# mLSTM's values and output gate as seven block products, with block differences of the normed activations kept in scratch

## The chip, the core and the metric

The kernel runs on one NeuronCore of a Trainium2 chip. Its engines work side by side, each through its own list of instructions in a fixed order: TensorE (PE in the profile, with PEld for the loading of its stationary operand), VectorE (DVE), ScalarE (ACT), GpSimd (POOL) and SyncE (SP, which here only issues DMA transfers). The metric is the device time of one execution in microseconds; the time of a kernel is the median of its runs.

## The reference

A decoder trunk of two layers over 512 tokens of width 1024, in float32. Each layer:

```
h = rmsnorm(x) * norm_mix
z = h @ w_in      # q, k, v of attention | q, k, v, o of mLSTM | i, f | gates A, B
att = sliding_window_attention(rope(qk_norm(q)), rope(qk_norm(k)), v)     # window 128
hm  = headnorm(mlstm(q_m, k_m, v_m, i, f)) * sigmoid(o_m)
x = x + (sigmoid(gA) * (att @ w_att_branch) + sigmoid(gB) * (hm @ w_m_branch)) @ w_out
x = x + relu(rmsnorm(x) * norm_ffn @ w_ff1)^2 @ w_ff2
```

`v_m` and `o_m` are each 512 wide, and their columns lie next to each other in `w_in` (`C_VM` 1280 and `C_OM` 1792). So h times these columns is one product of 512 x 1024 by 1024 x 1024.

## The kernel before

Every float32 operand of a projection is split into a high part, rounded to the matmul's float32r type, and a low part, the rest. `mm3` makes one product of three matmuls: high by high, high by low, low by high. Activations are split once (`norm.big`: two tiles of 128 x 8 x 512, features on the partitions). Weights are split chunk by chunk: `chunk` loads 128 rows by 512 columns on SP's queue into one of three raw buffers (`wraw`), ACT writes the high part (L195), DVE the low part (L196), into one of four pairs of buffers (`wsp`). `group_steps` turns a projection into 32 steps: 8 chunks times 4 output blocks of 128, three matmuls each, into four PSUM banks of 128 x 512. `banks` hands these out in pairs, named x, y and f, in turn. `tok_steps` leaves tokens on the output's partitions, `feat_steps` features.

The mixer of a layer is written as two `weave`s. A weave is a list of steps of matmuls, each with a width of 0.25 in a unit of its own (twelve matmuls make 1.0), and a list of side jobs with a position in that unit. Side jobs are attention, mLSTM, norms, transposes and `beat`s. The order on each engine is then fixed ahead of the run by a planner: it takes the work by priority as it expects it to be ready; `high_priority` brings a piece forward, and `issue_after` keeps it behind another on the same engine.

The first weave is attention's q, then its k and v with the gate logits (16 units). The second is, before: mLSTM's q and k (position 0), gates 0 and 1 (8 and 16), V with `ev_v` (24), the attention branch `a_steps` for both halves (32 and 36), gate 2 (40), O with `ev_o` (48), gate 3 (56 to 64). Attention's side jobs start at 7, one pair of query block and key head each 1.65. mLSTM's four heads start at 28 and each takes 4.65; `m_norm` follows, then `ev_o` multiplies the sigmoid of O into `hm`, and `head_tr` transposes and splits `hm` for the mLSTM branch, which comes behind the weave. The branches' product and `w_out` end the mixer.

`vm` holds V by token with a column of ones. It uses the buffer (`mid10`) of attention's keys `kT`. `xtok` holds x by token in four tiles of 128 x 2 x 512; the norm reads them at the mixer's start, and `ev_x` adds the mixer's result to them at its end.

The MLP makes most of its products by a scheme of seven block products: for a matrix product in 2 x 2 blocks, seven products of sums and differences of blocks stand in for eight. Sums of the weights' blocks are made by DMA in DRAM: class `Sums` copies one block with a DMA on ACT's queue (`copy`, L404) and adds another with an accumulating DMA on POOL's queue (`add`, L409, behind a small copy that marks the place, L407). These are jobs in a list; each `beat` sends one. The mixer's beats serve the MLP's sums of `w_ff2`.

Of the kernel before, what the change touches and what calls it, by code (L numbers as in the profile page):

```python
# [16 lines left out]
P = 128  # L17
# [18 lines left out]
def hybrid_kernel(ctx, tc, x, norm_mix, w_in, att_q_norm, att_k_norm, att_sinks, m_gate_bias,  # L36
# [39 lines left out]
    def temp(dt=F32):  # L76
        return now["tmp"].tile([P, T], dt, tag="t", name=nm("t"))
# [265 lines left out]
    xtok = [[const.tile([P, 2, T], F32, name=f"x{t}_{j}") for j in range(2)] for t in range(2)]  # L343
# [87 lines left out]
    def beats(*at):  # L431
        return [(a, beat) for a in at]

    def mixer(l, norm, late, order, phase):
# [20 lines left out]
        acts = norm.acts  # L455

# [7 lines left out]
        def ev_kv(b, ps):  # L464
# [5 lines left out]
              late + [(6.9, norm.columns), (10.0, lambda: row.append(norm.along()))])  # L470
# [283 lines left out]
        def ev_v(b, ps):  # L754
            if b == 0:
                vm.append(mid.tile([P, NB, MH, MV + 1], F32, tag="mid10", name=nm("vm")))
                gp.memset(vm[0][:, :, :, MV:], 1.0)
            sc.activation(vm[0][:, b, :, 0:MV], ps.rearrange("p (h v) -> p h v", h=MH), AF.Copy,
                          scale=norm.col[:, b:b + 1])
# [94 lines left out]
        side.append((28 + 4.65 * (MH + 1) + -0.55, m_norm))  # L854
# [4 lines left out]
        def head_tr(f):  # L859
            ps = aux()  # L860
            for b in range(NB):
# [450 lines left out]
```

## Time and profile before

| | |
|---|---|
| median of three runs | 1319.54 us (1313.72, 1319.54, 1320.67) |
| the profiled execution | 1317.72 us |
| its span, first to last instruction | 1316.0 us |
| mean granted clock of TensorE | 0.997 |
| first mixer's attention, mLSTM, branches | about 60 to 290 us of the span |
| first MLP | about 290 to 650 us |
| matmuls | 7126 |

The page shows shares of busy time, the chain of work that ended last, and groups of instructions by line. A matmul's duration in a group is longer than its share of TensorE's time, since a matmul begins before the one ahead of it has ended. Names such as mm<-i,wh say what is written and read: mm is a PSUM tile of a projection, i the split activations, wh and wl the parts of a weight chunk, aux a PSUM tile of attention, mLSTM or a transpose; a, t and u are buffers that several tensors use in turn, so mm<-u,wh in a mixer is the attention branch.

### The profile page before, as it was taken

How to read it: one execution, taken by the hardware profiler on the slowest of the kernel's cores; microseconds unless marked ns; L12 is line 12 of the kernel's file. 1: busy time of each engine (PE TensorE's matmuls, PEld its weight loads, DVE VectorE, ACT ScalarE, POOL GpSimd, SP SyncE). 2: the span in 40 equal slices, each digit the busy share in tenths (PEclk: the TensorE clock that was granted, in tenths of full speed). 3: DMA queues.
4: the chain of work that ended last, by engine and by line, in shares of the span. 5: the costliest groups of instructions: out<-in, count | busy, mean ns of one | idle time of the engine just before them, and what ended most of it. 6: DMA issues, size and time to landing. Idle time of an engine off the chain costs nothing.

```text
span 1316.0 us, 19614 instructions
## 1 busy us (share of the span) xinstructions
PE 1294.6 (98%) x7126; PEld 1112.5 (85%) x7126; DVE 967.1 (73%) x1507; ACT 782.5 (59%) x1393; POOL 228.8 (17%) x331
## 2 busy tenths in 40 slices
PE   9999999999999999999999999999999999999998
PEld 7877788888889989999888777888888899999987
DVE  4688764466578897978947887645757878979786
ACT  5568765544376656667544787564545766666663
POOL 4512311100011122220015023110001111213100
PEclk9999999999999999999999999999999999999999
DMA  5422136748287999776314222367483799997743
GB/s 153 111 71 72 57 101 153 178 129 241 59 199 184 265 181 221 189 176 199 104 35 122 63 75 63 105 154 174 135 241 52 189 239 229 185 258 147 190 145 128
DMA packets 139169, 196.52 MB, mean 149 GB/s; under 512 B 10424, under 2 KB 76576, under 8 KB 139072
## 3 DMA queue, kind: packets, MB, share of 16 engines
q1 hardware_dynamic: 93040, 135.88, 33.5%
q0 software_dynamic: 37568, 44.17, 22.0%
q10 hardware_dynamic: 8464, 15.21, 3.6%
q8 instruction: 56, 0.92, 0.3%
q14 instruction: 41, 0.34, 0.1%
HBM read 193.14 MB, written 31.46 MB: 171 GB/s over the span
## 4 chain that ended last, share of the span: by engine, by line
PE 82%; DVE 7%; issue 5%; DMA 3%; ACT 2%; POOL 0%; DVEq 0%; SPq 0%; POOLq 0%; ACTq 0%
PE mm L47 70%; PE aux L47 10%; DMA raw<-in_w_ff_dram 3%; PE aux L51 2%; DVE wl L196 2%; DVE t L646 1%; DVE t L696 1%; DVE wl L921 0%; ACT t L659 0%; ACT wh L195 0%; DVE t L623 0%; DVE a L725 0%; DVE a L876 0%; ACT wh L920 0%; DVE a L728 0%
## 5 line engine op out<-in xcount | busy, mean ns | idle before, releaser
L47 PE MATMUL mm<-i,wh 128*128 128x512 f32 (+1 forms) x1216 | 328.0, 357 | 4.6 <-DVE u L1153 4.6
L921 DVE TENSOR_TENSOR wl<-raw,wh 128x1024 fp32r<-128x1024 f32 x218 | 264.8, 1222 | 69.1 <-ACT wh L920 68.8
L920 ACT ACTIVATE wh<-raw 128x1024 fp32r<-128x1024 f32 x218 | 230.0, 1056 | 126.5 <-PE mm L47 57.2
L47 PEld LDWEIGHTS mm<-i,wh 128*128 128x128 f32 x1216 | 212.9, 192 | 31.3 <-DVE u L1153 5.0
L196 DVE TENSOR_TENSOR wl<-w,wh 128x512 fp32r<-128x512 f32 (+1 forms) x208 | 142.1, 684 | 119.3 <-ACT wh L195 111.9
L47 PE MATMUL mm<-i,wl 128*128 128x512 f32 (+1 forms) x608 | 215.5, 355 | 0.0
L195 ACT ACTIVATE wh<-w 128x512 fp32r<-128x512 f32 (+1 forms) x208 | 127.2, 612 | 145.2 <-PE mm L47 109.0
L47 PE MATMUL mm<-wh,uh 128*128 128x512 f32 x448 | 175.0, 391 | 0.0
L47 PE MATMUL mm<-wl,uh 128*128 128x512 f32 x448 | 174.8, 390 | 0.0
L47 PE MATMUL mm<-wh,ul 128*128 128x512 f32 x448 | 174.3, 389 | 0.0
L961 POOL DMA_DIRECT2D raw<-in_w_ff_dram x56 | 72.7, 1298 | 489.4 <-DVE wl L921 284.2
L47 PE MATMUL mm<-wh,i 128*128 128x512 f32 (+1 forms) x512 | 149.2, 369 | 0.2 <-ACT wh L195 0.2
L47 PEld LDWEIGHTS mm<-i,wl 128*128 128x128 f32 x608 | 116.6, 192 | 15.2
L47 PE MATMUL mm<-hs,wh 128*128 128x256 f32 x672 | 122.2, 283 | 0.3 <-ACT u L1149 0.3
L47 PEld LDWEIGHTS mm<-hs,wh 128*128 128x128 f32 x672 | 105.7, 192 | 1.7 <-ACT u L1149 0.5
L47 PEld LDWEIGHTS mm<-wh,i 128*128 128x128 f32 x512 | 91.5, 188 | 15.7 <-issue 0.7
L47 PEld LDWEIGHTS mm<-wh,ul 128*128 128x128 f32 x448 | 84.1, 188 | 18.0
L47 PEld LDWEIGHTS mm<-wh,uh 128*128 128x128 f32 x448 | 84.3, 188 | 16.3
L47 PEld LDWEIGHTS mm<-wl,uh 128*128 128x128 f32 x448 | 84.3, 188 | 16.0
L47 PE MATMUL mm<-hs,wl 128*128 128x256 f32 x336 | 95.1, 283 | 0.0
L47 PE MATMUL mm<-wl,i 128*128 128x512 f32 (+1 forms) x256 | 94.0, 367 | 0.0
L975 DVE SCALAR_TENSOR_TENSOR x<-mm,ninv,x 128x512 f32<-128x512 f32 x112 | 80.2, 747 | 18.5 <-PE mm L47 18.4
(246 smaller groups left out, 2198.1 us busy)
## 6 DMA issues: line engine op xcount, KB each, us to landing
raw<-in_w_ff_dram SPq DMA_DIRECT2D x124, 512.0 KB, 5.8
w<-in_w_in_dram SPq DMA_DIRECT2D x128, 256.0 KB, 2.7
raw<-in_w_ff_dram POOLq DMA_DIRECT2D x56, 512.0 KB, 7.2
sum<-in_w_ff_dram ACTq DMA_DIRECT2D x28, 512.0 KB, 5.0
raw<-sum SPq DMA_DIRECT2D x28, 512.0 KB, 4.2
sum<-in_w_ff_dram POOLq DMA_DIRECT2D x20, 512.0 KB, 6.4
w<-in_w_out_dram SPq DMA_DIRECT2D x32, 256.0 KB, 3.5
w<-in_w_att_branch_dram SPq DMA_DIRECT2D x16, 256.0 KB, 2.7
```

What stands on the lines that cost most here:

```text
L47: return nc.tensor.matmul(*args, **kw)
L51: return nc.tensor.transpose(*args)
L195: last_wh[:] = sc.activation(wh[:, :off], raw[:, :off], AF.Copy), wh
L196: ve.tensor_tensor(wl[:, :off], raw[:, :off], f32(wh[:, :off]), op=ALU.subtract)
L646: ve.copy_predicated(dst, tri_i.unsqueeze(1).to_broadcast([P, 2, P]), p4[:, :, 1, :])
L696: ve.tensor_tensor(b3[64 * i:64 * i + 64], p4[:, :, i, :], l4[:, :, i, :], op=ALU.add)
L920: last_wh[:] = sc.activation(hi, r, AF.Copy), hi[:, 0, :]
L921: ve.tensor_tensor(lo, r, f32(hi), op=ALU.subtract)
L961: nc.gpsimd.dma_start(r, w1_block(k, n, c0), accum_op=ALU.add)
L975: ve.scalar_tensor_tensor(xh[:, i, :], ps[i], norm.inv[:, 0 if sign > 0 else 1, b:b + 1], xh[:, i, :], op0=ALU.mult, op1=ALU.add)
```

## The change

V and O of a layer become one product in 2 x 2 x 2 blocks: two blocks of 256 tokens, two of 512 features, two of 512 columns (V and O). Seven block products take the place of eight. In the order in which they run they are 1, 2, 4, 5, 6, 7, 3. Each has four chunks of weights, two token blocks of 128 and three matmuls, that is 24 matmuls and a width of 2 in the weave; together 14 in the place of V (24 to 38), and O's place behind gate 2 is gone. Weights of 1, 2 and 3 are plain blocks; those of 4 to 7 are sums from DRAM, made by a `Sums` of its own in 16 jobs. Products 1, 2 and 4 take blocks of the split activations as they are. 5, 6, 7 and 3 take differences, which `left_steps` makes on DVE during the first weave and splits again on ACT and DVE. Those of 5 and 6 are kept in x's own tiles, those of 7 and 3 are written to DRAM by POOL and fetched into x's tiles when 5 and 6 are done. x itself comes back by four loads (`x_back`) from position 42.5, in layer 0 from the input, in layer 1 from copies in DRAM that POOL writes at the mixer's start.

The results add up in PSUM where they can (6 and 7 go on top of 1, 3 on top of 5) and otherwise in SBUF: `ev_vo` copies with ACT or adds with DVE. O's raw values wait in `oraw`, and `o_gate` takes their sigmoid behind `m_norm`. mLSTM's heads start at 32 instead of 28, and `head_tr` at 57.0.

```diff
-    xtok = [[const.tile([P, 2, T], F32, name=f"x{t}_{j}") for j in range(2)] for t in range(2)]
+    xpool = ctx.enter_context(tc.tile_pool(name="xpool", bufs=1, reuse_waits="tile"))
+
+    def x_tile(t, j, dt=F32):
+        return xpool.tile([P, 2, T], dt, tag=f"x{t}_{j}", name=nm(f"x{t}_{j}"))
+
+    xtok = [[x_tile(t, j) for j in range(2)] for t in range(2)]
...
+    def plan_vo(l):
+
+        s = Sums(l, 0, lambda l, _, i, j, h: w_in[l, T * i + 2 * P * h:T * i + 2 * P * (h + 1),
+                                                  C_VM + T * j:C_VM + T * (j + 1)])
+        jobs.extend(s.copies("DB") + s.adds("D") + s.copies("C") + s.adds("B") + s.copies("A") + s.adds("CA"))
+        return s
...
+        def x_back(t, j):
...
+            xtok[t][j] = x_tile(t, j)
+            nc.sync.dma_start(xtok[t][j], src)
...
+        if l:
+            for t in range(2):
+                for j in range(2):
+                    x_kept[t, j] = dram.tile([P, 2, T], F32, tag=nm("x"), name=nm("x"))
+                    gp.dma_start(x_kept[t, j], xtok[t][j])
+
+        def left_steps(at):
...
+            def whole(t, k):
+                r[t, k] = [temp(), temp()]
+                for d, (hi, lo) in zip(r[t, k], block(t, k)):
+                    ve.tensor_tensor(pair(d), f32(hi), f32(lo), op=ALU.add)
+
+            def keep(which, e):
+                if which in (5, 6):
+                    to = vo_left[which] = x_room(which)
+                    for n in range(2):
+                        h, lo = (v[:, 2 * n:2 * n + 2, :] for v in to)
+                        sc.activation(h, pair(r[e][n]), AF.Copy)
+                        ve.tensor_tensor(lo, pair(r[e][n]), f32(h), op=ALU.subtract)
+                    return
+                vo_left[which] = dram.tile([2, P, 2, T], F32, tag=nm("left"), name=nm("left"))
+                for n in range(2):
+                    hl = split(r[e][n], get=lambda: temp(F32R))
+                    for m in range(2):
+                        gp.dma_start(vo_left[which][m, :, n, :], f32(hl[m]))
...
+            return [(at, lambda: (whole(*a21), whole(*a22), minus(a22, a22, a21))), (at + 1, lambda: keep(5, a22)),
+                    (at + 2, lambda: (whole(*a11), minus(a22, a22, a11, -1.0))), (at + 3, lambda: keep(6, a22)),
+                    (at + 4, lambda: (minus(a21, a11, a21), keep(7, a21))),
+                    (at + 5.5, lambda: (whole(*a12), minus(a12, a22, a12, -1.0), keep(3, a12)))]
...
-              late + [(6.9, norm.columns), (10.0, lambda: row.append(norm.along()))])
+              late + [(6.9, norm.columns), (10.0, lambda: row.append(norm.along()))] + left_steps(7.2)
+              + beats(*(5 + 1.4 * n for n in range(8))))
...
+        def ev_vo(t, j, ps, add):
...
+            with tc.high_priority():
+                for i in range(2):
+                    b = 2 * t + i
+                    dst, src = oraw[t][:, i, :] if j else vm[0][:, b, :, 0:MV], ps[i]
...
+                    by = (mcol if j else norm.col)[:, b:b + 1]
+                    if add:
+                        ve.scalar_tensor_tensor(dst, src, by, dst, op0=ALU.mult, op1=ALU.add)
+                    else:
+                        sc.activation(dst, src, AF.Copy, scale=by)
+
+        def vo_steps():
+
+            ps, lefts = {}, {}
+            slots = [(1, "x", True, ((0, 0, False),)), (2, "z", True, ((0, 0, True),)),
+                     (4, "y", True, ((1, 0, False),)), (5, "z", True, ((1, 1, False),)),
+                     (6, "x", False, ((0, 1, False),)), (7, "x", False, ((1, 0, True), (1, 1, True))),
+                     (3, "z", False, ((0, 1, True),))]
...
+            def run(s, which, bank, fresh, evacs, kt, i, w):
...
+                mm3(ps[bank][i], ah[:, kt % 2, c], al[:, kt % 2, c], w[0], w[1], fresh and kt == 0, False,
+                    skip_group_check=True)
+                if kt == 3 and i == 1:
+                    for t, j, add in evacs:
+                        ev_vo(t, j, ps[bank], add)
+                    if which == 4:
+                        turn_of[0] -= 2
+                    elif which in (5, 6):
+                        fetch({5: 7, 6: 3}[which])
...
-        def ev_o(b, ps):
-            so = temp()
-            sc.activation(so, ps, AF.Sigmoid, scale=norm.col[:, b:b + 1])
-            ve.tensor_tensor(hm[b], hm[b], so, op=ALU.mult)
-            if b == NB - 1:
-                sigmoid(g2)
+        def o_gate():
+            for b in range(NB):
+                so = oraw[b // 2][:, b % 2, :]
+                sc.activation(so, so, AF.Sigmoid)
+                ve.tensor_tensor(hm[b], hm[b], so, op=ALU.mult)
+            sigmoid(g2)
...
-            at = 28 + 4.65 * h
+            at = 32 + 4.65 * h
...
-        side += [(57.75 + 1.25 * f, lambda f=f: head_tr(f)) for f in range(MH)]
+        side += [(57.0 + 1.1 * f, lambda f=f: head_tr(f)) for f in range(MH)]
...
-        side += beats(*(42 + 1.8 * n for n in range(12)))
-        weave(feat_steps(acts, wcols(C_QM, 512), ev_qk) + s0 + s1 + tok_steps(acts, wcols(C_VM, 512), ev_v)
-              + a_steps(0, g0) + a_steps(1, g1) + s2 + tok_steps(acts, wcols(C_OM, 512), ev_o) + s3, side)
+        side += [(42.5 + 2 * n, lambda n=n: x_back(n // 2, n % 2)) for n in range(4)]
+        side += beats(*(0.75 + 1.6 * n for n in range(8)), *(42 + 1.7 * n for n in range(12)))
+        weave(feat_steps(acts, wcols(C_QM, 512), ev_qk) + s0 + s1 + vo_steps()
+              + a_steps(0, g0) + a_steps(1, g1) + s2 + s3, side)
```

More of the change, by code (lines that the diff above doesn't have):

```diff
@@ L455, in mixer, with pair, block, x_room @@
         acts = norm.acts
+        vo_sums = plan_vo(l)
+        vo_left = {}
+        def pair(t):
+            return t.rearrange("p (k t) -> p k t", k=2)
+        def block(t, k):
+            return [tuple(b[:, 4 * k + 2 * n:4 * k + 2 * n + 2, 2 * P * t:2 * P * (t + 1)] for b in norm.big)
+                    for n in range(2)]
+        def x_room(which):
+            t = int(which in (6, 3))
+            return [x_tile(t, j, F32R).rearrange("p i (k t) -> p (i k) t", k=2) for j in range(2)]
@@ L752, in mixer @@
         vm = []
[L754 to L755 removed]
+        oraw = []
+        mcol = sm([P, NB], "mcol", 1)
+        ve.tensor_scalar(mcol, norm.col, -1.0, None, op0=ALU.mult)
+        def ev_vo(t, j, ps, add):
+            if not vm:
                 vm.append(mid.tile([P, NB, MH, MV + 1], F32, tag="mid10", name=nm("vm")))
                 gp.memset(vm[0][:, :, :, MV:], 1.0)
[L758 to L759 removed]
+            if j and not oraw:
+                oraw.extend(mid.tile([P, 2, T], F32, tag=tag, name=nm("o")) for tag in ("mid4", "kvi"))
+            with tc.high_priority():
+                for i in range(2):
+                    b = 2 * t + i
+                    dst, src = oraw[t][:, i, :] if j else vm[0][:, b, :, 0:MV], ps[i]
+                    if not j:
+                        src = src.rearrange("p (h v) -> p h v", h=MH)
+                    by = (mcol if j else norm.col)[:, b:b + 1]
+                    if add:
+                        ve.scalar_tensor_tensor(dst, src, by, dst, op0=ALU.mult, op1=ALU.add)
+                    else:
+                        sc.activation(dst, src, AF.Copy, scale=by)
```

43 lines of the change are left out of this document (42 added, 1 removed).

## The prediction

> **What bounds the kernel now.** I read the page's share of engines first, then the chain that ended last, then stretches of layer 0's mixer.
>
> ```profile
> span 1316.0 us, 19614 instructions
> PE 1294.6 (98%) x7126; PEld 1112.5 (85%) x7126; DVE 967.1 (73%) x1507; ACT 782.5 (59%) x1393; POOL 228.8 (17%) x331
> ...
> PE 82%; DVE 7%; issue 5%; DMA 3%; ACT 2%; POOL 0%; DVEq 0%; SPq 0%; POOLq 0%; ACTq 0%
> ```
>
> TensorE is busy in nearly all of the span and holds 82% of the chain; DVE holds 7%. What a matmul costs is not its mean of about 390 ns in the groups, since matmuls overlap. It is the step from one to the next, and a stretch of the chain without waits gives it (start, length, what):
>
> ```profile
> 230.34 20.45 PE mm L47 x90
> ```
>
> 20.45 / 90 = 0.2272 us for a 128x512 matmul. A projection of 96 such costs 21.8 us.
>
> Now the stretches, cut at the events that matter: the K/V stage and the attention's preparation (33 to 60), attention (60 to 163), mLSTM (163 to 230), the rest of the mixer.
>
> ```profile
> core 0: us, PE busy (x) PEld busy (x) DVE busy (x) ACT busy (x) POOL busy (x), PEclk, DMA share, GB/s
> 33.00:60.00 27.00, 27.00 (x166) 24.29 (x165) 17.92 (x41) 12.87 (x27) 13.07 (x22) 1.00 0.45 122
> 60.00:163.00 103.00, 98.34 (x480) 76.19 (x479) 84.98 (x204) 74.17 (x195) 28.58 (x53) 1.00 0.24 67
> 163.00:230.00 67.00, 66.97 (x342) 56.49 (x341) 37.88 (x111) 41.25 (x119) 9.79 (x22) 1.00 0.48 124
> 230.00:290.00 60.00, 60.00 (x276) 49.67 (x275) 33.27 (x58) 29.59 (x47) 3.72 (x6) 1.00 0.58 152
> ```
>
> From 163 on TensorE never waits, and DVE works 57% of the time. From 60 to 163 TensorE idles 4.7 us, and DVE is busy 84.98 / 103 = 82.5%. There the chain runs through attention, in turns on TensorE and DVE. Its end, and what TensorE does then:
>
> ```profile
> 156.73 0.69 DVE wl L196
> 157.43 0.67 DVE t L208
> 158.21 0.76 POOL t L680
> ...
> 160.32 1.19 PE aux L47 x4
> ...
> 163.73 5.03 PE mm L47 x22
> ...
> 165.42 0.39 PE L47 MATMUL mm<-wh,i 128*128 128x512 f32 x1
> 165.65 0.62 PE L47 MATMUL mm<-u,wh 128*128 128x512 f32 x2
> ```
>
> The last attention outputs are multiplied at 160 to 161, and the first matmul that reads them, `a_steps(0)` (mm<-u,wh), starts at 165.65, straight behind V's last one. So attention is done just before it is needed. That place decides this change.
>
> **The change, part by part (each layer).**
>
> *Matmuls.* V and O were 2 x 96 = 192; seven block products of 4 x 2 x 3 = 24 make 168. 24 x 0.2272 = **5.45 us less**, 10.9 in both layers. All are still 128x512 with a 128x128 stationary block.
>
> *Moved.* O's 96 matmuls leave the place behind mLSTM; 72 more stand ahead of `a_steps(0)`. TensorE reaches that point 72 x 0.2272 = 16.4 us later, at 182.0, and has 21.8 us less behind it. The layer comes out even if `a_steps(0)` starts at 165.65 + 21.8 = 187.5, better before, worse after.
>
> *DVE work added.* Prices:
>
> ```profile
> L196 DVE TENSOR_TENSOR wl<-w,wh x26: 652/692/1020, 59.9 to 156.7; 128x512 fp32r<-128x512 f32 x26
> L876 DVE TENSOR_TENSOR a<-a,a 128x512 f32<-128x512 f32 x16 | 11.0, 685 | 0.0
> L975 DVE SCALAR_TENSOR_TENSOR x<-mm,ninv,x x112: 740/747/757, 391.6 to 1312.2; 128x512 f32<-128x512 f32 x112
> L728 DVE TENSOR_TENSOR a<-a,a x8: 684/846/1025, 107.5 to 764.4; 64x512 fp32r<-64x512 f32 x8
> ```
>
> The left blocks: 8 sums, 8 differences and 8 low parts, 24 x 0.70 = 16.8 us, from weave position 7.2 of the first weave, about 33 us. Weight chunks: 28 instead of 16, and 20 more of them before `a_steps(0)`: 20 x 0.692 = 13.8. Evacuations that add: 8 x 0.747 = 6.0. Together 36.6 us before that point. From 33 to 60 DVE has 27 - 17.9 = 9.1 idle, so 7.7 of the left blocks spill into attention. From 60 to the start of `a_steps(0)` DVE then has 85.0 + 7.7 + 13.8 + 6.0 = 112.5 us to do. By 182.0 there are 122: a share of **92%**, against 82.5% now. The even point, 187.5, needs 88%.
>
> Can DVE do 92% beside a busy TensorE? In another stage it does more:
>
> ```profile
> 400.00:410.00 10.00, 10.00 (x68) 9.24 (x67) 10.00 (x11) 5.96 (x7) 1.55 (x2) 1.00 0.90 171
> ```
>
> That stage has simple chains; attention has not. But what is added (chunk splits, sums of blocks) hangs on no attention step and can fill DVE's 18 us of idle there. I take 0.5 us of new TensorE wait a layer. The ends: 4.7 us gained (the idle of today filled by the extra matmuls) and 9 us lost (below). The row of L728 shows one more price: the same form takes 684 to 1025 ns. If a third of the 24 left-block operations took the longer time, 8 x 0.34 = 2.7 us would be added to DVE's load, and the share by 182 would be 94%.
>
> The Trainium skill ("SBUF — State Buffer", section "SBUF: two separate sides") says why it could: VectorE with two SBUF inputs and a GpSimd operation that reads SBUF take one shared port pair in turn, the later one waiting for the whole instruction. All left-block operations have two SBUF inputs. The spread of L728 agrees.
>
> *ACT.* 12 splits, 8 high parts, 4 more copies out of PSUM:
>
> ```profile
> L195 ACT ACTIVATE wh<-w 128x512 fp32r<-128x512 f32 x26 | 16.3, 627 | 6.4 <-issue 2.7 <-PE mm L47 1.6 <-ACT t L659 0.7
> L758 ACT ACTIVATE vm<-mm,ncol x8: 682/690/698, 164.5 to 819.1; 128x512 f32<-128x512 f32 x8
> L404 ACTq DMA_DIRECT2D sum<-in_w_ff_dram x28: 497/497/589, 189.9 to 1099.6; - x28
> ```
>
> 20 x 0.63 + 4 x 0.69 = 15.4 us, and 8 copies of sums issued at 0.5 each, 4.0, on an engine busy 48% (33 to 60) and 72% (60 to 163). Covered: nothing. If ACT lagged, a chunk would be late by one 0.63.
>
> *A new wait.* Product 7 goes into the same banks as product 6, right behind it, so its first matmul waits for ACT's copy. Queued behind it on TensorE are the rest of the product, then `a_steps`. The price lies between 0 (mLSTM matmuls stand between) and 0.69 + 0.39 - 0.23 = 0.85 for one bank; the second copy hides behind three matmuls. I take 0.8. Products 2, 5 and 3 share banks too, but a product lies between.
>
> *A second new wait.* Product 1 is written to `vm`, whose buffer is the attention keys' until the last scores are made; today's first write comes at V's end. The last scores are read at 150.5, V begins at 130.1 (start, length, what):
>
> ```profile
> 150.50 0.46 DVE t L646
> ...
> 130.13 0.40 PE L47 MATMUL mm<-wh,i 128*128 128x512 f32 x1
> ```
>
> The banks hold products 1, 2 and 4; product 5 needs 2's, and with it ACT's and DVE's copies out. TensorE gets there after 72 matmuls: at V's pace of today (96 in 165.6 - 130.1 = 35.5) 26.6 us on, 156.7. The scores, 7.7 late with DVE's spill, end at 158.7, the copies 0.69 + 2 x 0.747 later: 160.9. Between 0 and 4.2, less what attention's matmuls fill, which are queued there anyhow: I take 0.3.
>
> *Loads.* SP issues 28 chunks, 4 fetches and 4 `x_back`; POOL 8 adds, 8 marks and 8 block writes, in layer 1 also 4 copies of x.
>
> ```profile
> w<-in_w_in_dram SPq DMA_DIRECT2D x128, 256.0 KB, 2.7
> ...
> raw<-sum SPq DMA_DIRECT2D x28, 512.0 KB, 4.2
> ...
> w<-in_w_out_dram SPq DMA_DIRECT2D x32, 256.0 KB, 3.5
> ...
> L409 POOL DMA_DIRECT2D sum<-in_w_ff_dram x20: 605/846/952, 202.6 to 1146.9; - x20
> ...
> 18.53 117.60 SPq L185 DMA_DIRECT2D w<-in_w_in_dram  x48
> 138.93 31.25 SPq L185 DMA_DIRECT2D w<-in_w_att_branch_dram  x8
> 320.00:330.00 10.00, 10.00 (x50) 8.31 (x49) 6.42 (x8) 6.09 (x14) 0.00 (x0) 1.00 1.11 326
> ```
>
> A chunk now feeds 6 matmuls, 1.36 us, instead of 2.73. With three raw buffers a chunk's load and split, 2.7 + 0.63 + 0.69, repeat every 4.02 / 3 = 1.34 us: just even. Beside more traffic a landing may take up to `w_out`'s 3.5, which makes 1.61 (28 x 0.25 = 7 a layer), or midway 1.47 (28 x 0.11 = 3.1). But the last V load is issued by 136.1 for a product that ends at 165.4: loads run far ahead, and attention's matmuls stretch the pace. I take 0, between 0 and 7. A fetch on SP waits for its product's last matmul, and the chunks queued behind it wait too; those of the next product are issued by then, if they run ahead as V's did, and one product (5.45) covers one landing of 4.2, two at once hardly. Bytes more: chunks 3, sums 4 + 4, blocks 2 + 2, x 2 make 17 MB a layer, over 150 us 113 GB/s on top of 67 to 124, under the 326 seen. POOL's issues cost 24 x 0.85 = 20 us on an engine busy 48% (33 to 60) and 28% (60 to 163); most fall ahead of the first scores, some ahead of masks (0.76 each) that attention waits for. For K/V chunks behind a block sum and for POOL and fetches together I take 0.2, between 0 and 3.
>
> *Tail.* mLSTM starts four positions later, and 24 instead of 32 chunks of 12 matmuls (2.73 us) stand behind the start of `a_steps(0)`: 24 x 2.73 = 65 us and its own matmuls. Today it needs 163 to 230, 67. The new gate pass (4 sigmoids at 0.62 beside 4 products at 0.69) ends before `hmT` is needed. Cost 0, at most 3.
>
> *Sum a layer:* -5.45 + 0.5 + 0.8 + 0.3 + 0.2 = -3.65; both: -7.3. The profiled execution took 1317.72 us around its span of 1316.0; 1317.7 - 7.3 = 1310.4, **1310**. The median shown, 1319.54, lies 1.8 above that execution; the runs spread from 1313.72 to 1320.67. About 0.5% (6.6 us) is what a measurement of this kernel can tell from no change.
>
> **Rivals.**
>
> *A, the forecast:* 1304 to 1314, chance 0.48. For it: TensorE holds the chain, and 163 to 290 has no wait to give back.
>
> *B, given back:* DVE reaches only 88 to 90%, `a_steps(0)` waits until 185 to 188: 112.5 / 0.89 = 126.4, 186.4, 187.5 - 186.4 = 1.1 better a layer, and the 0.8 of the bank wait eats most of it. 1317, range 1314 to 1321, chance 0.22. For it: attention's chain turns on DVE.
>
> *C, slower:* DVE stays at 82.5%. 112.5 / 0.825 = 136.4; `a_steps(0)` starts at 196.4 instead of 187.5, +8.9 a layer, **1335**; it decides from a share under 88%. Against it: the 18 us of idle. Chance 0.18, spread from 1324 to 1336.
>
> The Trainium skill ("Perfetto Trace Analysis", section "Identifying the Most-Contended Engine") judges TensorE by its weight loads, not by matmul time. By that, DVE (84.98) stands above PEld (76.19) in 60 to 163, which is C.
>
> *D, loads:* the chunk pace of 1.47 binds: -3.65 + 3.1 = -0.55 a layer, 1317; chance 0.05. Against it: no TensorE wait of 60 to 163 shows a load.
>
> *E, better:* the extra matmuls fill today's 4.7 us of idle in place of the 0.5 lost: -3.65 - 5.2 = -8.85 a layer, 1300; chance 0.07.
>
> That the matmuls don't go is no real case: the count is written out.
>
> **How the numbers follow.** Faster by over 0.5% means under 1311.1: E and 0.35 of A, 0.42. Within: the rest of A (0.13), B, D: 0.40. Slower: C, 0.18. Range 1302 to 1328: it leaves out most of E and the upper half of C, some 0.15, and of B and D nothing.
>
> **What would show it.** 7078 matmuls. DVE's share from 60 to the first mm<-u,wh, and that start: near 183 (A), 187 (B), 195 (C). A gap of 0.8 between products 6 and 7, ended by ACT. TensorE without waits behind it. The prediction is wrong if that start lies past 187.5, or if TensorE waits for chunks in the V and O stage or for `hmT` at its end.

## The result, and the profile after

The changed kernel takes **1352.55 us** (median of four runs, 1351.20 to 1354.76), against 1320.11 for the kernel before in the same comparison: a ratio (of the means) of 1.026, with a 95% interval of 1.0237 to 1.0282. It is slower by 32 us by the medians, by 34 by the ratio. The forecast was 1310, the range 1302 to 1328: the sign was wrong, and the range didn't hold the time. One slow execution of the kernels below, 4501 us in f1, is left out of that kernel's median and ratio.

The page of the changed kernel, its line of spans, its shares of engines, and of the chain:

```profile
span 1351.7 us, 19900 instructions
PE 1301.5 (96%) x7078; PEld 1112.0 (82%) x7078; DVE 1027.3 (76%) x1597; ACT 819.1 (61%) x1450; POOL 261.5 (19%) x383
...
PE 70%; issue 9%; DVE 7%; DMA 7%; ACT 4%; POOL 2%; SPq 0%; DVEq 0%; ACTq 0%; POOLq 0%
```

There are 7078 matmuls, as predicted, 48 fewer. But TensorE holds 70% of the chain instead of 82%, and DMA 7% instead of 3%. TensorE's busy time even rose, by 6.9 us; its clock explains that (last section).

To see where the time went, I take four dates in each layer: the first attention scores, the last attention outputs (aux<-t,v), `a_steps(0)` (the first mm<-u,wh) and the first matmul of the mLSTM branch (mm<-a,wh), which closes the part of the mixer that the change touches. In us of the span, from the timelines of TensorE:

```
                     layer 0                           layer 1
                     scores  outputs  a_steps  branch  scores  outputs  a_steps  branch
before                 65.4    160.3    165.7   269.5   717.8    812.7    818.0   921.9
after                  81.0    190.7    210.1   291.6   750.5    857.6    872.8   956.8
```

At the mLSTM branch layer 0 is 22.1 us late. Layer 1 adds 12.8 (956.8 - 921.9 - 22.1). That is nearly the whole loss, 34.9 of the 35.7 between the spans. In layer 0 the kernel is 15.6 late before attention has begun. From `a_steps(0)` to the mLSTM branch the time is 81.5 instead of 103.9: the 21.8 us that O took really left that place.

The windows of the changed kernel (us, busy time by engine, granted clock, DMA share, GB/s), from the K/V stage on:

```profile
33.00:60.00 27.00, 23.55 (x137) 20.55 (x136) 18.30 (x32) 12.23 (x25) 12.66 (x19) 0.94 0.87 218
60.00:210.10 150.10, 133.56 (x602) 103.22 (x601) 118.96 (x273) 100.44 (x246) 43.49 (x83) 0.93 0.49 139
```

Two things differ from the rows of before. From 33 to 60 the DMA engines are busy 87% instead of 45%, and TensorE, which never waited there, makes 137 matmuls instead of 166. From 60 to `a_steps(0)`, DVE is busy 118.96 / 150.10 = 79.3%. The prediction had wanted 88% for no loss.

The chain of work from 40 to 100 shows what stood in the way (start, length, what):

```profile
39.41 9.05 DMA w<-in_w_in_dram
...
55.82 5.16 DVE wl L196
...
67.45 0.62 POOL rp L652
```

In the kernel before, the chain's longest piece there is TensorE at work:

```profile
39.92 20.17 PE mm L47 x112
```

The changed kernel waits 9 us for one weight chunk, then for a subtraction of 5.16 us on DVE that takes 0.69 elsewhere, then for norms and rotary steps of q and k (L627 to L657). The waits of the changed kernel from 40 to 100 (who <- whom: us in all, times, longest) give the sizes:

```profile
ACT wh L195 <- DMA w<-in_w_in_dram: 18.4, 7, 6.6
POOL mark L412 <- ACT wh L195: 11.5, 2, 9.7
...
PE aux L51 <- POOL a L657: 6.2, 1, 6.2
POOL rp L652 <- DVE kvi L649: 6.1, 1, 6.1
```

POOL's timeline shows the second line of these at its place (start, length, line, operation, in brackets the idle time before it and what ended it):

```profile
51.73 0.63 POOL L412 COPY mark<-wh 1x2 f32<-1x2 f32 x1 [9.69 <-ACT wh L195]
52.31 0.90 POOL L414 DMA_DIRECT2D sum<-sum  x1
52.91 2.46 POOL L517 DMA_DIRECT2D left<-t  x4
55.12 4.31 POOL L626 TENSOR_TENSOR t<-a 128x512 f32<-128x512 f32 x4
59.12 1.30 POOL L629 TENSOR_TENSOR t<-kvi 128x512 f32<-128x512 f32 x1
...
67.45 0.62 POOL L652 TENSOR_TENSOR rp<-kvi,ct 128x32 f32<-128x32 f32 x1 [6.07 <-DVE kvi L649]
```

The same two steps in the kernel before:

```profile
47.60 1.04 POOL L553 TENSOR_TENSOR t<-kvi 128x512 f32<-128x512 f32 x1 [9.59 <-ACT kvi L465]
52.04 0.63 POOL L576 TENSOR_TENSOR rp<-kvi,ct 128x32 f32<-128x32 f32 x1 [3.40 <-DVE kvi L573]
```

The mark of a block sum waits 9.7 us for a weight chunk whose own load is late. Behind it in POOL's fixed order stand an accumulating DMA, four writes of differences, and then the squares of q and k (L626, L629). The last square is at 59.12 instead of 47.60, the first rotary step at 67.45 instead of 52.04.

### The profile page after: what moved, and what is told of

Read it like the earlier page. It is cut to its first block, busy times and chain, and to the rows that moved or that the text cites. A ratio compares the mean times of both kernels' runs of the same rounds, so it can differ in the third digit from the quotient of the medians.

```text
span 1351.7 us, 19900 instructions
## 1 busy us (share of the span) xinstructions
PE 1301.5 (96%) x7078; PEld 1112.0 (82%) x7078; DVE 1027.3 (76%) x1597; ACT 819.1 (61%) x1450; POOL 261.5 (19%) x383
## 3 DMA queue, kind: packets, MB, share of 16 engines
q1 hardware_dynamic: 99312, 150.56, 35.7%
## 4 chain that ended last, share of the span: by engine, by line
PE 70%; issue 9%; DVE 7%; DMA 7%; ACT 4%; POOL 2%; SPq 0%; DVEq 0%; ACTq 0%; POOLq 0%
PE mm L47 59%; PE aux L47 10%; DMA w<-in_w_in_dram 3%; DMA raw<-in_w_ff_dram 3%; DVE wl L196 2%; PE aux L51 2%; ACT wh L195 1%; DMA w<-in_w_att_branch_dram 1%; ACT t L735 1%; POOL rq L655 0%; DVE t L208 0%; POOL rp L652 0%; DVE t L699 0%; DVE t L772 0%; DVE t L722 0%
## 5 line engine op out<-in xcount | busy, mean ns | idle before, releaser
L47 PE MATMUL mm<-i,wh 128*128 128x512 f32 (+1 forms) x1216 | 334.0, 362 | 6.6 <-DVE u L1297 6.1
L196 DVE TENSOR_TENSOR wl<-w,wh 128x512 fp32r<-128x512 f32 (+1 forms) x232 | 167.7, 727 | 107.7 <-ACT wh L195 104.7
L47 PEld LDWEIGHTS mm<-i,wh 128*128 128x128 f32 x1216 | 215.9, 195 | 35.0 <-DVE u L1297 6.5
L195 ACT ACTIVATE wh<-w 128x512 fp32r<-128x512 f32 (+1 forms) x232 | 142.1, 614 | 155.9 <-PE mm L47 80.4
L47 PE MATMUL mm<-wh,i 128*128 128x512 f32 (+1 forms) x352 | 101.4, 366 | 7.1 <-ACT wh L195 6.2
L47 PE MATMUL mm<-wh,a 128*128 128x512 f32 x256 | 81.7, 393 | 0.5 <-DVE a L1019 0.5
L47 PE MATMUL aux<-i,wh 128*128 128x256 f32 x448 | 81.7, 283 | 0.0
```

The lines of the kernel that those rows point to most:

```text
L47: return nc.tensor.matmul(*args, **kw)
L195: last_wh[:] = sc.activation(wh[:, :off], raw[:, :off], AF.Copy), wh
L196: ve.tensor_tensor(wl[:, :off], raw[:, :off], f32(wh[:, :off]), op=ALU.subtract)
```

## The experiments

All ratios are against the kernel before, run on the same chip in the same batch (medians 1316.79 for e1 to e4, 1319.49 for f1 to f4, 1318.15 for the last four). In microseconds I multiply by 1318. If nothing were lost, the 48 matmuls fewer would give -10.9 us, a ratio of 0.9917.

**First batch: which part costs?** My theory after the result: loads and POOL's list ahead of attention cost most, DVE's added work the rest.

*e1, no sums.* The 16 DMA jobs of the sums go; products 4 to 7 read plain blocks of the weights (so the values aren't V and O).

```diff
-        jobs.extend(s.copies("DB") + s.adds("D") + s.copies("C") + s.adds("B") + s.copies("A") + s.adds("CA"))
...
-              + beats(*(5 + 1.4 * n for n in range(8))))
+              )
...
-                    plain = {1: (0, 0), 3: (1, 1), 2: (1, 0)}.get(which)
+                    plain = {1: (0, 0), 3: (1, 1), 2: (1, 0), 4: (1, 0), 5: (0, 1), 6: (0, 0), 7: (0, 1)}.get(which)
...
-        side += beats(*(0.75 + 1.6 * n for n in range(8)), *(42 + 1.7 * n for n in range(12)))
+        side += beats(*(42 + 1.7 * n for n in range(12)))
```

> The changed kernel without the sums of V's and O's weight blocks: products 4 to 7 read plain blocks, and the 16 copies and adds with their marks are left out. Matmuls, chunk count, left blocks and scratch stay. Theory T (transfers: the sums and the scratch fill the DMA engines from 33 to 75 us, weight chunks land late, and POOL reaches attention's preparation late): most of the loss is the sums', 1325 to 1338, the stage from the first K/V matmul to the second weave back from 17.7 to under 13.5 us. Theory D (DVE: the added 36 us of work ahead of the attention branch): little changes, 1344 to 1353.

Measured: 1330.93 us, 1.0099 (1.0073 to 1.0125), as theory T had it. The sums cost (1.0260 - 1.0099) x 1318 = 21 us. From the first to the last K/V matmul (128x264) TensorE takes 12.4 us, instead of 17.4 in the changed kernel and 11.3 before.

*e2, no scratch.* The differences for 7 and 3 are made and split, but not written to DRAM or fetched; these products read those of 5 and 6.

```diff
-                vo_left[which] = dram.tile([2, P, 2, T], F32, tag=nm("left"), name=nm("left"))
                 for n in range(2):
-                    hl = split(r[e][n], get=lambda: temp(F32R))
-                    for m in range(2):
-                        gp.dma_start(vo_left[which][m, :, n, :], f32(hl[m]))
+                    split(r[e][n], get=lambda: temp(F32R))
...
-                to = vo_left[which]
-                if which in (3, 7):
-                    to = x_room(which)
...
+                to = vo_left[{7: 5, 3: 6}.get(which, which)]
```

> The changed kernel without the scratch in DRAM: the differences for products 7 and 3 are made and split but not written nor fetched, and these products read the blocks of 5 and 6. Theory T: part of the loss goes, 1338 to 1348, less than without the sums, since the writes are 2 MB a layer against some 12. The stall at the V and O stage's end goes too. Theory D: 1346 to 1353.

Measured: 1342.71, 1.0194 (1.0179 to 1.0210), as theory T had it: the scratch costs 9 us.

*e3, neither.* Both edits. All of DVE's added work is still there.

> Both left out: no sums, no scratch. DVE and ACT do the same work as in the changed kernel, with x moved away and back. Theory T: within 5 us of the kernel before, 1312 to 1325. Theory D: 1340 to 1352.

Measured: 1325.14, 1.0061 (1.0046 to 1.0076). Sums and scratch together cost 26 us, more than three quarters of the loss. What is left still stands 19 us above 0.9917; the time lies at the upper end of T's range, far below D's.

*e4, products only.* Besides, `left_steps` goes (24 operations of DVE a layer), and all moves of x: the seven products read the split activations as they are.

```diff
-              late + [(6.9, norm.columns), (10.0, lambda: row.append(norm.along()))] + left_steps(7.2)
+              late + [(6.9, norm.columns), (10.0, lambda: row.append(norm.along()))]
...
-            for which, e in ((1, (0, 0)), (2, (0, 1)), (4, (1, 1))):
+            for which, e in ((1, (0, 0)), (2, (0, 1)), (4, (1, 1)), (5, (1, 1)), (6, (0, 0)), (7, (1, 0)), (3, (0, 1))):
...
-        side += [(42.5 + 2 * n, lambda n=n: x_back(n // 2, n % 2)) for n in range(4)]
```

> Only the matmuls' new form: no sums, no left blocks (products 5, 6, 7 and 3 read plain blocks of the activations), x stays. 168 matmuls, 28 chunks and the adding evacuations remain. Theory T: the saving of 10.9 us shows nearly whole, 1308 to 1314, and 4 to 10 us below the run without sums and scratch. Theory D: 1312 to 1325, and 20 us or more below that run, since the left blocks' 17 us of DVE a layer are gone.

Measured: 1320.60, 1.0026 (1.0016 to 1.0035). The left blocks and the moves of x cost (1.0061 - 1.0026) x 1318 = 4.6 us. Neither theory had this: T wanted 1308 to 1314, D 20 us from the left blocks alone. With 48 matmuls fewer, no sums, no differences and no scratch, the kernel still isn't faster than before: 14 us are lost to something that every form of the change has.

**Second batch: the two waits, and the place of the sums.** In e4's timeline of TensorE both waits that the prediction had named appear:

```profile
155.07 0.50 PE L47 MATMUL mm<-wh,i 128*128 128x512 f32 x1 [1.05 <-DVE vm L847]
...
167.75 0.39 PE L47 MATMUL mm<-wh,i 128*128 128x512 f32 x1
...
170.53 1.27 PE L47 MATMUL aux<-t,v 128*128 128x512 f32 x4 [1.57 <-POOL t L753]
...
176.35 0.79 PE L47 MATMUL mm<-wh,i 128*128 128x512 f32 x1 [0.93 <-ACT o L849]
```

The first is product 5 behind the copies into `vm`, 1.05 us. The last is product 7 behind ACT's copies of product 6 (L849). TensorE stood idle for 0.93 right ahead of it, but product 6 had ended at 168.14 (167.75 + 0.39). ACT made the copies from 175.03 on, behind attention's last operations in its list, and so products 7 and 3, 48 matmuls, came to lie behind attention's end. Two kernels take these waits away.

*f1, swap.* e4 with product 3 ahead of 7, so that a product with banks of its own follows 6.

```diff
-                     (6, "x", False, ((0, 1, False),)), (7, "x", False, ((1, 0, True), (1, 1, True))),
-                     (3, "z", False, ((0, 1, True),))]
+                     (6, "x", False, ((0, 1, False),)), (3, "z", False, ((0, 1, True),)),
+                     (7, "x", False, ((1, 0, True), (1, 1, True)))]
...
+                    elif which == 7:
+                        turn_of[0] -= 1
```

> The run with products only (no sums, no left blocks, products 5, 6, 7 and 3 on plain blocks), now with product 3 between 6 and 7, so that no product writes the banks of the one before it; gates and branch take their banks in turn behind it. Theory B (bank hand-over: in layer 0 the end of attention stood alone on TensorE because product 7 waited for ACT's copy of 6, and the idle halved the clock for 10 us): 6 to 12 us faster than products only, 1309 to 1315. Theory D (DVE's chunk splits hold attention up): no change, 1318 to 1323.

Measured: 1323.84 (median of nine), 1.0041 (1.0026 to 1.0056). No gain, so theory B fails. `a_steps(0)` of layer 0 starts 6.6 us earlier than in e4 (185.1 for 191.7), but the last attention outputs come 1.3 later, and the mLSTM branch starts at 272.9 for 273.1.

*f2, columns.* f1 with O's columns first, so that products 1 and 2 go to free tiles, not to `vm`.

```diff
-                                                  C_VM + T * j:C_VM + T * (j + 1)])
+                                                  C_VM + T * (1 - j):C_VM + T * (2 - j)])
...
-                    dst, src = oraw[t][:, i, :] if j else vm[0][:, b, :, 0:MV], ps[i]
+                    dst, src = vm[0][:, b, :, 0:MV] if j else oraw[t][:, i, :], ps[i]
```

> The same, and O's columns first, V's second, so that products 1 and 2 are copied into a buffer that is free and not into V's, which waits for the last scores. Theory B: another 1 to 3 us (the wait of 1.0 us before product 5 in layer 0 and what it halves of the clock), 1307 to 1313. Theory D: as the run before it.

Measured: 1331.07, 1.0093 (1.0071 to 1.0115): slower, outside the ranges of both theories. TensorE runs through the products as it should, with `a_steps(0)` only 2.8 us behind the last attention outputs (18.4 in e4). But those now come at 184.7 instead of 173.3. My reading is that the earlier a product runs, the earlier DVE must split its chunks, and attention waits for DVE instead; no run isolates it.

*f3, late sums.* The whole change, with all 16 sum jobs in the second weave.

```diff
-              + beats(*(5 + 1.4 * n for n in range(8))))
+              )
...
-        side += beats(*(0.75 + 1.6 * n for n in range(8)), *(42 + 1.7 * n for n in range(12)))
+        side += beats(*(0.75 + 1.3 * n for n in range(16)), *(42 + 1.7 * n for n in range(12)))
```

> The whole change with one edit: the first 8 of the 16 sum jobs are sent in the second weave (all 16 from position 0.75, 1.3 apart) instead of the first. The same bytes and issues, elsewhere. Theory T (place: they collide with the K/V chunks and the left blocks' writes): the K/V stage is back within 2 us, 1335 to 1343. If the bytes as such cost the time, wherever they run, or POOL's issues do: 1348 to 1356.

Measured: 1339.44, 1.0155 (1.0132 to 1.0178). The sums cost 14 us less here; the first scores are at 73.5 instead of 81.0, and the K/V matmuls take 12.4 us, as in e1. The first mark still stands ahead of the rotary steps in POOL's order, with the DMA engines busy ahead of it:

```profile
33.00:60.00 27.00, 25.54 (x155) 22.45 (x154) 20.28 (x49) 14.88 (x32) 11.10 (x15) 1.00 0.79 247
```

*f4, all.* f3 with the orders of f1 and f2 (and products 3 and 7 changing rooms, `fetch({5: 3, 6: 7}[which])`).

> The whole change with the three edits together: late sums, product 3 between 6 and 7 (their scratch in the other pair of x's tiles), O's columns first. Theories T and B: 1320 to 1332, by adding the gains. It beats the kernel before only if the scratch costs nothing any more.

Measured: 1335.11, 1.0132 (1.0100 to 1.0164), above the range expected, and 3 us below f3, within the two intervals. No gain from the order of the products shows with the whole change either.

**Third batch: DVE's share, and the sums later still.** In every kernel so far DVE was busy 78 to 82% of the time from 60 to `a_steps(0)`, which is rival C. If that is the bound, taking DVE work away must pay, and adding as much to the kernel before must cost.

*g1, no low parts.* e4 without DVE's part of the splitting of the V and O chunks; the second matmul of each three reads the high part instead of the low. The number of matmuls stays.

```diff
-            wl = now["wsp"].tile([P, T], F32R, tag="wl", name=nm("wl"))
+            wl = None if low == "none" else now["wsp"].tile([P, T], F32R, tag="wl", name=nm("wl"))
...
+                if low == "none":
+                    return wh, wh
...
-                    w[:] = chunk([src])
+                    w[:] = chunk([src], low="none")
```

> The run with products only (no sums, no left blocks), and the 28 chunks of V and O a layer without their low part: DVE's subtraction is left out and the low matmul reads the high part. Matmuls, loads and ACT's splits stay. Theory D (attention runs at the pace of DVE, which is busy 79 to 82% of the time from 60 us to the attention branch in all kernels so far; 19 us of 105 go): the branch starts at 172 to 182 instead of 191.7 in layer 0, the whole takes 1303 to 1311. If ACT's splits or the loads set that pace: 1316 to 1322.

Measured: 1312.19, 0.9952 (0.9937 to 0.9966). The 28 subtractions a layer are worth (1.0026 - 0.9952) x 1318 = 9.8 us in all, and the time lies 1 us above theory D's range. In layer 1, where the clock is whole in e4 and g1 alike up to `a_steps(0)`, g1 is 3.5 us ahead; the 7.3 of layer 0 hold 10.2 us at half clock in e4 as well (last section). This is the only kernel of the study below the kernel before, and it leaves out part of the computation.

*g2, low parts on POOL.* e4 with every second low part of these chunks on POOL (`low=gp if kt % 2 else None`).

> Products only, with the low part of every second chunk of V and O made by POOL instead of DVE: the same work, 9.7 us of it moved from DVE to an engine busy 23%. Theory D: about half of the gain of the run without low parts, 1308 to 1316. If POOL's operations hold DVE up, or POOL comes late with them: 1318 to 1330.

Measured: 1323.82, 1.0041 (1.0028 to 1.0055). In layer 0 it helps, the mLSTM branch starts at 270.0 instead of 273.1; layer 1 gives it back, 925.4 for 925.5. No gain in all: the time lies in the range for POOL holding DVE up or coming late, and which of the two was not tried.

*h1, the kernel before with more for DVE.* 20 operations of 128x512 a layer, 13.8 us by L196's 0.69, at positions 12 to 31 of the second weave. Nothing else is changed.

```diff
+        def more():
+            with tc.high_priority():
+                ve.tensor_tensor(junk, f32(last_wh[1]), f32(last_wh[1]), op=ALU.add)
+
+        side += [(12 + n, more) for n in range(20)]
```

> The kernel before with 20 DVE operations of 128x512 more a layer, each reading the newest weight chunk's high part, one per chunk from position 12 to 31 of the second weave (their result is never used). That is the DVE work of the 20 chunks that the change has more ahead of the attention branch; matmuls, loads and ACT are as before. Theory D: 13.8 / 0.82 = 17 us a layer later at the branch, less what today's slack takes: 1338 to 1354. If DVE has room there: 1316 to 1328.

Measured: 1335.81, 1.0127 (1.0104 to 1.0150): 16.7 us for 27.6 of DVE work. It lies between the two ranges: DVE hasn't the room, but theory D's price was too high. By the dates it is 9.5 in layer 0 and 10.0 in layer 1. The same stretch, from 60 to `a_steps(0)`, in the kernel before, h1, e4 and g1:

```profile
60.00:165.60 105.60, 100.94 (x491) 78.40 (x490) 86.59 (x209) 76.70 (x202) 29.24 (x54) 1.00 0.24 67
```

```profile
60.00:173.30 113.30, 103.02 (x491) 79.80 (x490) 97.07 (x223) 77.32 (x200) 30.11 (x55) 0.96 0.25 68
```

```profile
60.00:191.70 131.70, 123.02 (x569) 94.81 (x567) 104.98 (x241) 96.44 (x237) 30.67 (x56) 0.96 0.32 90
```

```profile
60.00:185.00 125.00, 119.94 (x579) 93.97 (x577) 88.37 (x219) 99.46 (x252) 31.37 (x64) 1.00 0.36 99
```

DVE's busy time in them (the third engine) is 82.0, 85.7, 79.7 and 70.7% of the stretch. TensorE's is 95.6, 90.9, 93.4 and 96.0%. Where DVE's load is raised, the stretch grows and TensorE waits more; in g1, with 16.6 us less of it than e4, TensorE stands idle for 5.1 us, about as before (4.7). h1's 9.5 us in layer 0 have two parts: it stands idle for 10.3 us in this stretch, 5.6 more than before (4.1 of it in one wait for DVE), and the same 491 matmuls take 2.1 longer in it, the work behind it up to the mLSTM branch 1.8, since the clock is halved for 10.2 us, beginning in that wait.

*f5, sums behind the rotary steps.* The whole change, with the 16 jobs of f3 at `6.5 + 1.15 * n`.

> The whole change with all 16 sum jobs between positions 6.5 and 23.75 of the second weave, behind the rotary operations on POOL that the first scores wait for. Against the run with sums from 0.75 on (1339): if POOL's marks and issues ahead of the rotary operations cost the first scores their 7 us, 1326 to 1334; if it is the bytes or the left blocks, 1336 to 1344.

Measured: 1327.57, 1.0064 (1.0041 to 1.0086): 26 us better than the change as it was, in the range for POOL's marks and issues, and as good as e3, which has neither sums nor scratch. Its K/V matmuls take 12.4 us, as f3's. Its row from 33 to 60, and how long the chunks' loads took from 20 to 80:

```profile
33.00:60.00 27.00, 26.08 (x158) 22.89 (x157) 23.36 (x55) 15.64 (x33) 12.76 (x17) 1.00 0.64 195
```

```profile
DMA to landing us min/median/max: 1.8/2.7/6.4
```

In the changed kernel the same view says:

```profile
DMA to landing us min/median/max: 1.9/3.4/10.3
```

and in the kernel before:

```profile
DMA to landing us min/median/max: 1.8/2.6/3.4
```

Layer 0's dates for all kernels (us of the span; the first scores of the five left empty lie at 65.4 to 66.4), and by how much the mLSTM branch is late in layer 0 and how much layer 1 adds:

```
                 ratio    scores  outputs  a_steps  branch   late in 0   layer 1 adds
before           1          65.4    160.3    165.7   269.5
after            1.0260     81.0    190.7    210.1   291.6     +22.1        +12.8
e1_no_sums       1.0099     69.1    178.7    197.1   278.5      +9.0         +3.1
e2_no_scratch    1.0194     75.4    189.4    208.1   289.5     +19.9         +5.3
e3_neither       1.0061     66.6    176.7    195.8   277.2      +7.7         +0.4
e4_products_only 1.0026     65.1    173.3    191.7   273.1      +3.6          0.0
f1_swap          1.0041             174.6    185.1   272.9      +3.4         +0.4
f2_swap_cols     1.0093             184.7    187.5   276.6      +7.0         +6.4
f3_late_sums     1.0155     73.5    182.8    201.3   282.8     +13.2         +7.1
f4_all           1.0132     73.6    192.3    193.3   279.1      +9.6         +6.2
f5_later_sums    1.0064     69.5    176.3    194.8   276.2      +6.6         +2.2
g1_no_low        0.9952             164.5    185.0   265.8      -3.7         -3.5
g2_low_pool      1.0041             169.2    188.0   270.0      +0.4         +3.1
h1_before_dve    1.0127             171.4    173.3   279.0      +9.5        +10.0
```

The column to read is "outputs". In the kernel before, the mLSTM branch starts 109.2 us behind the last attention outputs. In the changed forms that keep product 7's place it is 100 to 101: O's 96 matmuls there take 10.9 us longer than the 48 of two products, and the halved clock takes back a part. In these forms the last outputs less what layer 0 is late give 168 to 170, so the layer comes out even if they come by about 169. They come at 190.7 in the change and at 173.3 in e4.

No form that computes the whole beat the kernel before; f5 comes nearest.

## Why the prediction was wrong

By its own steps, in us a layer (the mean of the two), as predicted and as the runs show. Differences of ratios from two batches carry about 3 us in all, so 1.5 a layer.

```
step                                           predicted        shown
matmuls                                            -5.45        -5.45  (7078)
loads (sums, scratch, POOL's list)         0.2, 0 to 3          +13.1  after to e3
left blocks and moves of x            0.5, -4.7 to 9 in all      +2.3  e3 to e4
DVE: low parts of V and O's chunks        (in the same 0.5)      +4.9  e4 to g1
bank hand-over and vm                              0.8 + 0.3      not told apart: g1 to 0.9917
ACT, tail                                              0, 0       leaves +2.3 for all three
sum                                                -3.65        +17.1
```

The price of the low parts is taken from all 28 that g1 leaves out; up to `a_steps(0)` that is 16.6 us of the 18.4 that e4's DVE works more there than before (104.98 against 86.59), so it stands for nearly all of the added load. Each difference holds what the waits cost in clock as well.

**The step that failed is "Loads"**, "I take 0.2, between 0 and 3". It weighed bytes over 150 us: 113 GB/s on top of 67 to 124, "under the 326 seen". It even said that most of POOL's issues "fall ahead of the first scores". But they don't spread over 150 us: all 16 jobs of the sums and all 8 writes of the scratch are issued between 17 and 86, and in two stretches the DMA engines were full. The changed kernel in these, and f5 in the first of them:

```profile
40.00:50.00 10.00, 6.89 (x53) 6.47 (x52) 3.78 (x9) 0.97 (x3) 1.82 (x4) 0.96 1.01 318
60.00:70.00 10.00, 7.36 (x33) 5.72 (x31) 9.96 (x28) 3.21 (x8) 3.86 (x8) 0.99 1.04 316
...
40.00:50.00 10.00, 9.08 (x67) 8.40 (x66) 6.92 (x12) 4.72 (x10) 6.65 (x10) 1.00 0.93 309
```

318 GB/s is about the 326 that the prediction itself had quoted as seen, and in the first of these TensorE is busy 6.89 of 10. The rate alone doesn't tell: f5 moves 309 GB/s there with the scratch's writes and no sums, its weight chunks land in 5.7 us instead of 9.4 (256 KB, median of those issued from 40 to 50), and TensorE is busy 9.08. In the changed kernel the chunks' loads share the engines with transfers of twice their size too (issues of the changed kernel from 20 to 100: kind, count, KB each, median us to landing):

```profile
w<-in_w_in_dram SPq DMA_DIRECT2D x18, 256.0 KB, 4.2
sum<-in_w_in_dram ACTq DMA_DIRECT2D x7, 512.0 KB, 5.5
sum<-in_w_in_dram POOLq DMA_DIRECT2D x4, 512.0 KB, 7.7
left<-t POOLq DMA_DIRECT2D x8, 256.0 KB, 8.3
sum<-sum POOLq DMA_DIRECT2D x4, 512.0 KB, 6.8
```

A late chunk then holds up a mark, and the mark holds up POOL's squares and rotary steps. That it is the place and not the work is shown by f5: the same sums, the same scratch and the same bytes, with the jobs behind the rotary steps, cost nothing that can be measured over e3 (1.0064 and 1.0061). f3 is halfway there and costs halfway. How the 26 us divide between late chunks and POOL's order is shown only in part: f3 moved both at once, but its K/V matmuls take 12.4 us as f5's do, so the 12 us from f3 to f5 are not K/V chunks that came late.

**DVE.** The prediction asked "Can DVE do 92% beside a busy TensorE?" and argued that chunk splits can fill DVE's idle time since they hang on no attention step. They hardly can: in every changed kernel with the load DVE stays at 78 to 82%, and the stretch grows instead; in h1 it comes to 85.7%, and the stretch still grows by 7.7. My reading is that attention's chain turns on DVE again and again, and each operation put in between makes the next step of the chain late. h1 shows the cost without any of the change: 13.8 us of DVE work a layer, on which nothing waits, cost 8.4 by the ratio (9.5 and 10.0 by the dates of its profile). So rival C had the right mechanism, and the term was mis-sized, 0.5 for 7, though inside its bound of 9 (2.3 of the 7 with ACT's part of the left blocks and the loads of x). C's price was too high for layer 1: for e3, which has DVE's whole load and little else, C's sum gives 1335, and e3 took 1325.14; layer 0 was 7.7 late (C: 8.9), layer 1 only 0.4. Why layer 1 takes it better than h1's 10.0 was not tried. That the result lies past C's time is the work of the loads.

The spread that the prediction saw in L728 was there, and worse. From 55.82 DVE's subtraction takes 5.16 us, during POOL's four squares and the one behind them (55.12 to 60.42, quoted above). The Trainium skill ("SBUF — State Buffer", section "SBUF: two separate sides") says that VectorE with two SBUF inputs and a GpSimd operation that reads SBUF take one port pair in turn, the later blocked for the other's whole instruction. The trace agrees that it was blocked, but for five instructions in a row, not one. That is not the rule here: in f5 POOL makes the same five from 46.58 to 52.96, and three subtractions among them take 2.35 us (two) and 0.93.

**The two waits** are there, 0.93 and 1.05 us, near the 0.85 and within the 0 to 4.2 predicted. Removing them bought nothing (f1) or cost (f2, where attention ended 11 us later than in e4). The prices were near, but a wait of TensorE cost nothing here, where attention ended no earlier without it. The prediction also took it that all 72 extra matmuls would be done by 182, with `a_steps(0)` straight behind them; the hand-over put 48 of them behind the last attention outputs, and the even point belongs at these, about 169, not at `a_steps(0)`.

**Right:** the matmuls and their 5.45 us; O's place (103.9 to 81.5); the tail, at no cost: `hmT` was ready in time for the branch in both layers (from `a_steps(0)` the changed kernel takes 81.5 and 83.9 us). The test named for C, `a_steps(0)` past 187.5 with DVE's share unchanged, told A from C. In the changed kernel it is passed by far, 210.1, with the loads in it. e3, without them, starts at 195.8 where C had 196.4; that this is so near is in part luck, since DVE had 107.1 us to do there and not 112.5, at 78.9% and not 82.5.

## What to carry to other kernels

Judge added transfers by the 10 us in which they are issued and by how late the loads beside them land, not by the mean over a stage, and look at what stands behind each issue and each marker in its engine's order: moving 16 DMA jobs behind the rotary steps was worth 26 us. An engine that is busy 80% in a chain of short alternating steps can already be the bound, and work for it is not free, even if it hangs on no step of that chain; add the same number of dummy operations to the old kernel first, since that prices it without the rest of the change. A wait of the busiest engine is worth removing only if what it would run ahead to doesn't need the engine that holds the chain.

## What the runs showed of the hardware that was not expected

Waits cost TensorE its clock as well. In the changed kernel the mean granted clock is 0.983. That is 1351.7 x 0.017 = 23 us of clock, against 1316.0 x 0.003 = 4 in the kernel before, and it is why 48 matmuls fewer took more busy time. In h1 (clock 0.987) the same sum gives 17. Windows of 1 us around attention's end in the changed kernel (the clock is the third number from the end):

```profile
189.00:190.00 1.00, 0.74 (x1) 0.29 (x1) 0.62 (x3) 0.51 (x2) 0.93 (x3) 0.61 1.03 291
...
199.00:200.00 1.00, 1.00 (x5) 0.86 (x4) 0.69 (x1) 0.14 (x2) 0.30 (x2) 0.77 0.27 39
```

By the shares 0.61 and 0.77 the clock was half from 189.22 to 199.46, 10.2 us; TensorE had been idle for 1.84 when it began, as its timeline shows:

```profile
189.26 0.80 PE L47 MATMUL aux<-t,v 128*128 128x512 f32 x1 [1.84 <-POOL t L756]
```

In e4 the same happens from 171.44 to 181.68, again 10.2, behind an idle time of 1.57 (the row of 170.53 above). The Trainium skill ("TensorE: Matmul & The Clock Gate", section "🔬 Part 1: The HAM clock gate (the "warmup" mystery)") says that the clock goes to half after an idle window of about 3.4 us, and back after as long a busy one. The halved stretches of these traces last 3.4, 6.8 or 10.2 us, one, two or three such windows, so the size agrees; but the idle times ahead of the two stretches above, 1.84 us in the changed kernel and 1.57 in e4, are far below a window. In the kernel before one of 1.42 us had no such stretch behind it; its timeline, and the window with the clock:

```profile
79.40 0.30 PE L51 MATMUL aux<-ident,kvi 128*128 128x128 f32 x1 [1.42 <-DVE t L646]
```

```profile
79.00:80.00 1.00, 0.60 (x3) 0.51 (x4) 0.75 (x2) 0.54 (x2) 0.00 (x0) 1.00 0.56 137
```

Nor had one of 1.86 in e1, longer than those two, so the length of one idle time doesn't decide it; what does is not shown:

```profile
63.65 0.66 PE L51 MATMUL aux<-ident,a 128*128 128x128 f32 x4 [1.86 <-POOL a L656]
```

```profile
63.00:67.00 4.00, 3.35 (x17) 2.82 (x18) 1.40 (x4) 2.00 (x5) 3.84 (x14) 1.00 0.43 131
```

How much of the loss the clock makes was not measured by itself. The 23 us against 4 bound it: at most 19 of the 35.7 between the spans. The two stretches shown stand right behind a wait of TensorE, so the clock is a part of what such a wait costs.
